# Second attention: scores in two float32r passes over stacked halves, queries made ready once per token tile

## The chip, the cores and the metric

The kernel runs on one core of a Trainium2 chip. Its time is the device time of one execution in microseconds (us). The engines are TensorE (PE, with its weight loads shown apart as PEld), VectorE (DVE), ScalarE (ACT), GpSimd (POOL) and SyncE (SP, which issues most DMAs). PE's granted clock is near its upper level for the whole span (0.996 of 2.4 GHz).

## What is computed

Two transformer blocks follow each other on 512 tokens of 1024 features, all in float32: a first block (convolution, stick-breaking attention, attention over a memory, gates, MLP), then an attention layer, a gated feed-forward layer, a state-space layer, and another feed-forward layer. The change is in the attention layer of the second part, which has two kinds of eight heads of 64 each:

```
    qa = rmsnorm(heads(qa, H_A), q_norm_a)
    ka = rmsnorm(heads(ka, H_A), k_norm_a)
...
    oa = band_attention(qa, ka, heads(va, H_A), A_PREV_CHUNKS, bias_a, None)
    qb = rmsnorm(heads(qb, H_B), q_norm_b)
    kb = rmsnorm(heads(kb, H_B_KV), k_norm_b)
...
    bias_b = (-slopes[:, None, None] * jnp.abs(rel_b).astype(jnp.float32)).reshape(
```

Kind a sees all 512 tokens back, with a bias from a table; kind b sees a window of 128, with a bias of a slope 2^-(h+1) times the distance, a sink in the softmax's denominator, and one key head for four query heads.

## The kernel before

A Python program records every instruction in the order in which its engine will run it. It keeps a clock of its own, with estimated costs, and a heap of generators: each does a few instructions, yields a delay, and is taken up again when that time has come. Weight products are jobs (`jobB`), taken one after the other; between their matmuls `pump` runs what is due in the heap, so the attention's instructions land between the projections' matmuls. Each engine then runs its own queue strictly in order and waits on semaphores where data isn't ready. Weight matmuls (`gb`) take three float32r passes, over weights that ACT (`whi`) and DVE (`wlo`) split into a high and a low part.

The attention layer projects the shared keys and values of kind b, then the queries `qb`, then `ka`, `qa`, `va`, and at last two halves of the output projection for each kind. When a token tile (128 tokens) of a projection is done, `head_norm` (L1338) squares it (`sq`, ACT), sums, takes the root on POOL, scales into `ay` (DVE), has PE transpose it (`at`) and ACT copy it out with the gain (`qb`, `ka`, `qa`, `kbT`). Tiles hold two heads of 64 in 128 partitions.

`units_of` (L1399) makes one unit for each token tile and head, first all of kind b, then all of kind a; `Flow` starts one at least every 1.4 us of the recording's clock (`LA`), up to six at a time. A unit's steps: `sz` masks a pair's query tile into two tiles `qz`, each with the other head's 64 partitions zeroed (`by_head`, L206, on ACT or DVE, whichever the recording believes free); `s0` computes the scores `as` (PE, one float32 matmul) and adds bias and takes the row's minimum in one DVE instruction (`less`, `ae`); `s1` exponentials (ACT); `s2` the reciprocal and the scaling (DVE or ACT); `s3` transposes (`ap`, PE) and copies out (`apT`, ACT); `s4` multiplies with the values (`ao`, PE), whose result is split into `oTh` and `oTl` for the output projection. For kind b the bias table `relB` was multiplied by each head's slope ahead of time, eight ACT instructions into a tile of eight tables.

The first block's stick-breaking attention works otherwise already: `pair_evac` makes tiles `qq` and `kk` in which a head's high part lies in 64 partitions and its low part, or a copy, in the other 64, and its scores `z` are two float32r matmuls. Its rows in the trace are quoted below.

Of the kernel before, what the change touches and what calls it, by code (L numbers as in the profile page):

```python
# [21 lines left out]
KD = 8  # L22
# [21 lines left out]
COLS = {}  # L44
# [27 lines left out]
def kernel(ctx: ExitStack, tc: tile.TileContext, ins: dict, out: bass.AP, parts=(1, 2, 3, 4, 5)):  # L72
# [150 lines left out]
    halves = cp.tile([128, 2], F32, tag="halves", name="halves")  # L223
# [5 lines left out]
    def setup_consts():  # L229
# [3 lines left out]
        for i in range(2):  # L233
            dve.memset(halves[64 * i:64 * i + 64, i:i + 1], 1.0)
            dve.memset(halves[64 - 64 * i:128 - 64 * i, i:i + 1], 0.0)
# [1076 lines left out]
    def attn(G):  # L1312
# [4 lines left out]
        def less(e, s, bias, first, m):  # L1317

            dve.tensor_tensor_reduce(out=e, in0=s, in1=bias, scale=-1.0, scalar=first, op0=ALU.add, op1=ALU.min,
                                     accum_out=m)  # L1320

        def load_rel():
            relB = t2("relB")[:, 0:256]
# [5 lines left out]
            def heads():  # L1329
                dve.tensor_scalar(out=S["sink"], in0=col("sink", 0, 8), scalar1=-1.0, scalar2=None, op0=ALU.mult)  # L1330
                for h in range(8):
                    act.activation(out=S["relB"][:, h * 256:(h + 1) * 256], in_=relB, func=AF.Copy,
                                   scale=2.0 ** -(h + 1))
                    yield 0.6

            spawn(heads(), 4.0)

        def head_norm(src, nh, dst, tt, gname, dup, key):  # L1338
# [12 lines left out]
            dve.tensor_scalar(out=r, in0=r, scalar1=rs, scalar2=None, op0=ALU.mult)  # L1351
            y = t2("ay")
            rb = r.rearrange("p (h o) -> p h o", o=1).to_broadcast([128, nh, 64])
            if dup:
                for i in range(2):
                    dve.tensor_tensor(out=y[:, 0:2 * n].rearrange("p (h i d) -> p h i d", i=2, d=64)[:, :, i, :],
# [663 lines left out]
```

## Time and profile before

| what | us |
|---|---|
| median of 3 runs (2481.61 to 2482.71) | 2482.68 |
| the profiled execution's own time | 2481.79 |
| its span, first to last instruction | 2480.1 |
| PE busy | 2438.7 |
| DVE busy | 1527.0 |
| ACT busy | 1120.3 |

A busy time is the part of the span in which the engine had at least one instruction under way. Consecutive matmuls overlap in the trace: one starts before the end that is shown for the one before it, so a stretch is read from start to start. An idle time is put down to what released the engine.

### The profile page before, as it was taken

How to read it: one execution, taken by the hardware profiler on the slowest of the kernel's cores; microseconds unless marked ns; L12 is line 12 of the kernel's file. 1: busy time of each engine (PE TensorE's matmuls, PEld its weight loads, DVE VectorE, ACT ScalarE, POOL GpSimd, SP SyncE). 2: the span in 40 equal slices, each digit the busy share in tenths (PEclk: the TensorE clock that was granted, in tenths of full speed). 3: DMA queues.
4: the chain of work that ended last, by engine and by line, in shares of the span. 5: the costliest groups of instructions: out<-in, count | busy, mean ns of one | idle time of the engine just before them, and what ended most of it. 6: DMA issues, size and time to landing. Idle time of an engine off the chain costs nothing.

```text
span 2480.1 us, 30728 instructions
## 1 busy us (share of the span) xinstructions
PE 2438.7 (98%) x11556; PEld 1980.8 (80%) x11556; DVE 1527.0 (62%) x2784; ACT 1120.3 (45%) x2410; POOL 248.2 (10%) x303
## 2 busy tenths in 40 slices
PE   8999999999999999999999999999999999999999
PEld 6877877788888888888776888887788887888887
DVE  6436456653444566646756566776698687667674
ACT  6545444432333444545666343333565545433332
POOL 1102011101110011102100000000011011001010
PEclk9999999999999999999999999999999998999999
DMA  6313332333323565622221354442432431245452
GB/s 206 104 57 96 112 100 79 91 106 111 102 89 116 156 166 138 130 89 76 78 72 40 112 136 119 133 97 79 117 106 78 124 115 60 91 147 119 136 111 77
DMA packets 218533, 264.78 MB, mean 107 GB/s; under 512 B 7024, under 2 KB 157936, under 8 KB 218384
## 3 DMA queue, kind: packets, MB, share of 16 engines
q1 hardware_dynamic: 198848, 222.83, 27.9%
q0 software_dynamic: 15232, 29.36, 7.4%
q10 hardware_dynamic: 4304, 10.62, 1.5%
q8 instruction: 91, 1.49, 0.3%
q14 instruction: 58, 0.48, 0.1%
HBM read 254.33 MB, written 4.26 MB: 104 GB/s over the span
## 4 chain that ended last, share of the span: by engine, by line
PE 87%; DVE 5%; issue 4%; ACT 2%; DMA 1%; POOL 0%; ACTq 0%; SPq 0%; POOLq 0%; DVEq 0%
PE ga L87 47%; PE gb L87 21%; PE gw L87 11%; PE y L87 2%; PE as L87 1%; DVE wlo L120 1%; PE o L87 1%; PE tr L92 1%; PE aT L92 1%; PE z L87 1%; PE ao L87 1%; DVE fy L120 1%; PE ap L92 0%; DVE ae L120 0%; PE st L87 0%
## 5 line engine op out<-in xcount | busy, mean ns | idle before, releaser
L87 PE MATMUL ga<-hh,whi 128*128 128x512 f32 x1672 | 661.1, 395 | 0.0
L87 PE MATMUL ga<-hh,wlo 128*128 128x512 f32 x1672 | 652.2, 390 | 0.3 <-DVE wlo L120 0.2
L87 PE MATMUL ga<-hl,whi 128*128 128x512 f32 x1672 | 652.0, 390 | 0.0
L120 DVE TENSOR_TENSOR wlo<-raw,whi 128x512 fp32r<-128x512 f32 x701 | 479.3, 705 | 228.0 <-ACT whi L120 226.1
L120 ACT CAST whi<-raw 128x512 fp32r<-128x512 f32 x701 | 413.2, 617 | 157.2 <-PE ga L87 63.5
L87 PEld LDWEIGHTS ga<-hh,wlo 128*128 128x128 f32 x1672 | 313.6, 188 | 68.0 <-DVE wlo L120 1.2
L87 PEld LDWEIGHTS ga<-hh,whi 128*128 128x128 f32 x1672 | 313.9, 188 | 66.2 <-issue 2.6
L87 PEld LDWEIGHTS ga<-hl,whi 128*128 128x128 f32 x1672 | 314.0, 188 | 64.6 <-issue 1.2
L87 PE MATMUL gb<-whi,hh 128*128 128x512 f32 (+1 forms) x416 | 170.8, 411 | 0.0
L87 PE MATMUL gb<-wlo,hh 128*128 128x512 f32 (+1 forms) x416 | 159.0, 382 | 1.1 <-DVE wlo L120 1.1
L87 PE MATMUL gb<-whi,hl 128*128 128x512 f32 (+1 forms) x416 | 159.7, 384 | 0.0
L120 DVE TENSOR_TENSOR wlo<-b,whi 128x512 fp32r<-128x512 f32 x196 | 131.2, 686 | 36.8 <-ACT whi L120 36.8
L120 ACT ACTIVATE fy<-fy,cols 128x512 f32<-128x512 f32 x60 | 43.5, 725 | 206.5 <-DVE fy L120 206.4
L120 ACT CAST whi<-b 128x512 fp32r<-128x512 f32 x196 | 114.1, 615 | 15.6 <-PE gw L87 11.2
L120 DVE SCALAR_TENSOR_TENSOR x<-gw,rsp,x 128x512 f32<-128x512 f32 x98 | 70.0, 750 | 69.4 <-PE gw L87 69.2
L120 DVE SCALAR_TENSOR_TENSOR fy<-fg,cols,fy 128x510 f32<-128x510 f32 (+1 forms) x136 | 103.4, 760 | 4.8
L120 DVE TENSOR_TENSOR fg<-ga,R 128x512 f32<-128x512 f32 x68 | 46.8, 689 | 80.7 <-PE ga L87 69.8
L87 PEld LDWEIGHTS gb<-whi,hl 128*128 128x128 f32 x416 | 78.2, 188 | 16.0
L87 PEld LDWEIGHTS gb<-wlo,hh 128*128 128x128 f32 x416 | 78.5, 189 | 15.2 <-DVE wlo L120 1.7
L87 PEld LDWEIGHTS gb<-whi,hh 128*128 128x128 f32 x416 | 78.4, 188 | 14.2 <-issue 1.2
L655 POOL DMA_DIRECT2D b<-in_ffn_w_out_dram x32 | 38.5, 1203 | 507.6 <-DVE wlo L120 503.7
L87 PE MATMUL gw<-whi,fss 128*128 128x512 f32 x256 | 81.4, 389 | 0.0
(316 smaller groups left out, 4002.4 us busy)
## 6 DMA issues: line engine op xcount, KB each, us to landing
raw<-in_ffn_w_in_dram SPq DMA_DIRECT2D x44, 1024.0 KB, 5.1
raw<-in_w_in_dram SPq DMA_DIRECT2D x32, 1024.0 KB, 5.1
raw<-in_w_up_dram SPq DMA_DIRECT2D x16, 1024.0 KB, 5.5
b<-in_ffn_w_out_dram POOLq DMA_DIRECT2D x32, 512.0 KB, 5.6
raw<-in_ssm_w_in_dram SPq DMA_DIRECT2D x16, 1024.0 KB, 5.2
b<-in_w_down_dram POOLq DMA_DIRECT2D x24, 512.0 KB, 6.1
b<-in_ffn_w_out_dram SPq DMA_DIRECT2D x12, 1024.0 KB, 8.0
b<-in_w_down_dram SPq DMA_DIRECT2D x9, 1024.0 KB, 7.9
```

The source lines that it names most:

```text
L87: nc.tensor.matmul(o, lhsT=lhsT, rhs=rhs, **kw)
L92: nc.tensor.transpose(o, i, idn)
L120: return fn(*args, **kw)
L655: nc.gpsimd.dma_start(out=r3(R[nm][:, a * 512:(c + 1) * 512], c + 1 - a), in_=dram(i, j, a, c + 1), accum_op=ALU.add)
```

## The change

Scores of the second attention are computed in two float32r passes instead of one float32 matmul. The key tiles (`put_k`) hold, for each of the two heads, the high part in that head's 64 partitions (ACT) and the low part in the other 64 (DVE). The queries keep their transposed float32 tile (`put_q`), and a new generator `queries` makes, once for each token tile and kind, a tile `qq`: for each of the two heads ACT casts the high part, DVE subtracts to get the low part, and a DMA issued from ACT copies both into the other 64 partitions. It is spawned at the first unit of a kind for tile 0, and in the third head pair of a tile for the next; `s0` waits for it in the recording's clock. `by_head` and its masks go. The slopes of kind b move: `relB` is one table, the queries are multiplied by 2^(h+1) in the scaling that was there (by a tile `slope` set once by eight GpSimd memsets), and `less` multiplies the sum by -2^-(h+1) instead of -1. The key tile of kind b is no longer doubled ahead of its transposes (one transpose in place of two).

```diff
-    def by_head(q):
-
-        z = t2("qz")[:, 0:256]
-        for g in range(2):
-            o, h = z[:, g * 128:(g + 1) * 128], halves[:, g:g + 1]
-            if lighter(dve, act, 0.0) is act:
-                act.activation(out=o, in_=q, func=AF.Copy, scale=h)
-            else:
-                dve.tensor_scalar(out=o, in0=q, scalar1=h, scalar2=None, op0=ALU.mult)
-        return z
...
-            S["relB"] = u8("relB8")
...
+            S["slope"] = cp.tile([128, 8], F32, tag="slope", name="slope")
+            for h in range(8):
+                pool.memset(S["slope"][:, h:h + 1], 2.0 ** (h + 1))
...
+        def put_k(key):
+
+            def put(ps, tt):
+                for g in range(2):
+                    hi, lo = slice(64 * g, 64 * g + 64), slice(64 - 64 * g, 128 - 64 * g)
+                    t = r3(S[key][g], ps.shape[1])
+                    gain = cols[hi, COLS[key + "g"]:COLS[key + "g"] + 1]
+                    c = slice(tt * 128, tt * 128 + 128)
+                    act.activation(out=t[hi, :, c], in_=ps[hi], func=AF.Copy, scale=gain)
+                    dve.scalar_tensor_tensor(out=t[lo, :, c], in0=ps[hi], scalar=gain, in1=f(t[hi, :, c]),
+                                             op0=ALU.mult, op1=ALU.subtract)
+            return put
+
+        def queries(kind, tt):
+
+            while ("q" + kind, tt) not in S:
+                yield 0.3
+            t = u8("qq", F32R)
+            q = r3(S["q" + kind], 4)[:, :, tt * 128:tt * 128 + 128]
+            for g in range(2):
+                hi, lo = slice(64 * g, 64 * g + 64), slice(64 - 64 * g, 128 - 64 * g)
+                a = g * 1024
+                act.copy(r3(t[:, a:a + 512], 4)[hi], q[hi])
+                dve.tensor_sub(r3(t[:, a + 512:a + 1024], 4)[hi], q[hi], f(r3(t[:, a:a + 512], 4)[hi]))
+                act.dma_start(out=f(t[lo, a:a + 1024]), in_=f(t[hi, a:a + 1024]))
+            yield 3.0
+            S["qq" + kind, tt] = t
...
+        def score(ps, q, k, pr, g):
+            for i in range(2):
+                o = g * 1024 + i * 512 + pr * 128
+                pe.matmul(ps, lhsT=q[:, o:o + 128], rhs=k, start=i == 0, stop=i == 1)
...
-                        def sz(pr=pr, tt=tt, c=c, g=g):
-                            if g == 0:
-                                c["q"] = by_head(S["q" + kind][:, pr * 512 + tt * 128:pr * 512 + tt * 128 + 128])
+                        def sz(pr=pr, tt=tt, g=g):
+                            if g == 0 and pr == 0 and tt == 0:
+                                spawn(queries(kind, 0))
+                            if g == 0 and pr == 2 and tt < 3:
+                                spawn(queries(kind, tt + 1))
...
-                                pe.matmul(S_, lhsT=q, rhs=S["kb"][:, o:o + n], start=True, stop=True)
-                                less(e, S_, S["relB"][:, h * 256 + 256 - n:h * 256 + 256], S["sink"][:, h:h + 1], m)
+                                score(S_, q, S["kb"][pr // 2][:, t0 * 128:t0 * 128 + n], pr, g)
+                                less(e, S_, S["relB"][:, 256 - n:256], S["sink"][:, h:h + 1], m, 2.0 ** -(h + 1))
...
-            a = small("acol", 32)
+            a = t2("acol")[:, 0:32]
```

What moves is shown at three places. On PE at the start of kind b: `at` are the transposes of a query tile, `gb` the weight matmuls (here of the projection of `ka`), `as` the scores. Before, from the first tile's transposes on:

```order
L92 MATMUL at<-ident,ay 128x128 x4
L87 MATMUL gb<-whi_0_9857,hh_9322 128x512
L87 MATMUL gb<-wlo_0_9858,hh_9322 128x512
L87 MATMUL gb<-whi_0_9857,hl_9323 128x512
L87 MATMUL gb<-whi_1_9880,hh_9322 128x512
L87 MATMUL gb<-wlo_1_9881,hh_9322 128x512
L87 MATMUL gb<-whi_1_9880,hl_9323 128x512
L87 MATMUL as<-kbT,qz 128x128
```

Now twelve weight matmuls follow the first tile's transposes, and then, from the second tile's transposes on:

```order
L92 MATMUL at<-ident,ay 128x128 x4
L87 MATMUL gb<-whi_0_9857,hh_9317 128x512
L87 MATMUL gb<-wlo_0_9858,hh_9317 128x512
L87 MATMUL gb<-whi_0_9857,hl_9318 128x512
L87 MATMUL gb<-whi_1_9880,hh_9317 128x512
L87 MATMUL gb<-wlo_1_9881,hh_9317 128x512
L87 MATMUL gb<-whi_1_9880,hl_9318 128x512
L87 MATMUL as<-kb,qq 128x128 x6
```

The first score moved from behind 6 weight matmuls to behind 18 and another tile's transposes, and three heads' scores (two passes each) stand together there.

On ACT at the same place (`sq` are squares of later tiles, `whi` weight casts, `ae` exponentials; in brackets whom an instruction waits for). Before:

```order
L120 ACTIVATE qb<-at,cols 128x4x128 [waits PE_49]
L120 ACTIVATE sq<-gb,asc 128x512 [waits DVE_49]
L120 CAST whi_1_9994<-raw_9855 128x512 [waits Activation_49]
L120 ACTIVATE qb<-at,cols 128x4x128 [waits PE_49]
L120 ACT_TABLE_LOAD [waits DVE_49]
L120 ACTIVATE ae,sd<-ae,sm 128x128 [waits Activation_49]
```

Now:

```order
L120 ACTIVATE qb<-at,cols 128x4x128 [waits PE_49]
L120 ACTIVATE sq<-gb,asc 128x512 [waits DVE_49]
L120 CAST qq<-qb 64x512 [waits Activation_49]
L1377 DMA qq<-qq 64x1024 [waits DVE_49]
L120 CAST qq<-qb 64x512
L1377 DMA qq<-qq 64x1024 [waits DVE_49]
L120 CAST whi_1_9998<-raw_9855 128x512
L120 ACTIVATE qb<-at,cols 128x4x128 [waits PE_49]
```

Two casts and two DMAs stand ahead of the weight cast, and each DMA waits in ACT's queue for DVE.

On ACT at the start of kind a, around the first eviction of a value tile (`va`). Before:

```order
L120 ACTIVATE va<-gb,rs 128x512 [waits PE_49]
L120 ACTIVATE ae,sd<-ae,sm 128x128 [waits DVE_49]
L120 COPY apT<-ap 128x128 [waits PE_49]
L120 CAST oTh_10194<-ao 128x128 [waits PE_49]
L120 CAST whi_2_11274<-raw_10873 128x512
```

Now:

```order
L120 ACTIVATE va<-gb,rs 128x512 [waits DMAHW1_49,DMAHW0_49,PE_49]
L120 ACTIVATE ae<-ae,sd 128x256 [waits DVE_49,Activation_49]
L120 CAST qq<-qa 64x512
L1377 DMA qq<-qq 64x1024 [waits DVE_49]
L120 CAST qq<-qa 64x512
L1377 DMA qq<-qq 64x1024 [waits DVE_49]
L120 CAST whi_2_11225<-raw_10815 128x512
L120 COPY apT<-ap 128x256 [waits PE_49]
```

Kind a's first query tile is made behind the first value tile's eviction; before, kind a's first exponentials stood there already. On PE, 18 weight matmuls and eight small ones (four `ao`, four `ap`) stand between the end of that value tile and kind a's first scores.

## Rows read from the trace of the kernel before

**Rows 1.** The page's busy times, share of the span, and instructions.

```profile
PE 2438.7 (98%) x11556; PEld 1980.8 (80%) x11556; DVE 1527.0 (62%) x2784; ACT 1120.3 (45%) x2410; POOL 248.2 (10%) x303
```

**Rows 2.** Stretches: us, then busy PE, PEld, DVE, ACT, POOL; clock, DMA share, GB/s.

```profile
1164.00:1259.00 95.00, 93.82 (x533) 73.31 (x531) 68.29 (x274) 67.70 (x216) 16.96 (x10) 1.00 0.22 74
1259.00:1349.00 90.00, 83.43 (x490) 59.39 (x489) 51.58 (x192) 57.02 (x162) 0.00 (x0) 1.00 0.18 59
```

**Rows 3.** Groups by form, 1160 to 1350 us, score records: count, busy us, mean ns.

```profile
L87 PE MATMUL as<-kbT,qz 128*128 128x256 f32 x48 | 14.0, 386 | 1.2 <-DVE sd L120 1.1
L87 PE MATMUL as<-ka,qz 128*128 128x512 f32 x16 | 8.5, 612 | 0.6 <-ACT qz L120 0.6
...
L87 PE MATMUL as<-ka,qz 128*128 128x384 f32 x16 | 6.8, 505 | 1.3 <-ACT qz L120 1.3
L87 PE MATMUL as<-ka,qz 128*128 128x256 f32 x16 | 4.8, 384 | 0.0
```

**Rows 4.** Groups by form, 190 to 540 us: the first block's scores.

```profile
L87 PE MATMUL z<-kk,qq 128*128 128x512 f32 x32 | 11.0, 424 | 0.0
L87 PE MATMUL z<-kk,qq 128*128 128x384 f32 x32 | 9.0, 362 | 0.0
L87 PE MATMUL z<-kk,qq 128*128 128x256 f32 x32 | 6.5, 286 | 0.0
```

**Rows 5.** Timeline of PE, 1163 to 1167 us: start, us, instruction.

```profile
1163.41 0.60 PE L92 MATMUL at<-ident,ay 128*128 128x128 f32 x4
1163.76 0.48 PE L87 MATMUL gb<-whi,hh 128*128 128x512 f32 x1
```

**Rows 6.** Waits of PE, 1150 to 1350 us: total, times, longest.

```profile
PE gb L87 <- DVE oTl L120: 2.5, 3, 1.7
PE gb L87 <- ACT oTh L120: 2.2, 3, 1.0
PE as L87 <- ACT qz L120: 2.0, 3, 1.1
```

**Rows 7.** Timeline of ACT, 196 to 204 us: start, us, instruction, idle before.

```profile
196.33 0.59 ACT L120 ACTIVATE qq<-ga 64x512 fp32r<-64x512 f32 x1 [2.99 <-PE ga L87]
197.67 0.52 ACTq L1079 DMA_DIRECT2D qq<-qq  x1
198.24 0.59 ACT L120 ACTIVATE qq<-ga 64x512 fp32r<-64x512 f32 x1 [1.31 <-DVE qq L120]
199.59 0.47 ACTq L1079 DMA_DIRECT2D qq<-qq  x1
200.10 1.14 ACT L120 CAST whi<-raw 128x512 fp32r<-128x512 f32 x2 [1.27 <-DVE qq L120]
201.77 0.58 ACT L120 CAST kk<-ga 64x512 fp32r<-64x512 f32 x1 [0.53 <-PE ga L87]
203.11 0.58 ACT L120 CAST kk<-ga 64x512 fp32r<-64x512 f32 x1 [0.75 <-DVE kk L120]
203.71 0.62 ACT L120 CAST whi<-raw 128x512 fp32r<-128x512 f32 x1
```

**Rows 8.** Groups by form of ACT, 1130 to 1350 us: the masks.

```profile
L120 ACT ACTIVATE qz<-qa,halves 128x128 f32<-128x128 f32 x16 | 5.7, 395 | 0.0
L120 ACT ACTIVATE qz<-qb,halves 128x128 f32<-128x128 f32 x11 | 4.1, 400 | 0.0
```

**Rows 9.** The chain that ended last, 1160 to 1180 us: start, us, what.

```profile
1167.70 1.39 PE gb L87 x6
```

**Rows 10.** Timeline of ACT, 1163 to 1166 us.

```profile
1164.04 0.69 ACT L120 ACTIVATE qb<-at,cols 128x512 f32<-128x512 f32 x1 [1.96 <-PE at L92]
1164.63 0.68 ACT L120 ACTIVATE sq<-gb,asc 128x512 f32<-128x512 f32 x1
1165.20 0.62 ACT L120 CAST whi<-raw 128x512 fp32r<-128x512 f32 x1
```

**Rows 11.** DMA issues: count, KB each, us from issue to landing.

```profile
qq<-qq ACTq DMA_DIRECT2D x16, 256.0 KB, 2.9
```

**Rows 12.** Waits of ACT, 1164 to 1259 us: total, times, longest.

```profile
ACT apT L120 <- PE ap L92: 8.9, 9, 2.5
```

More of the change, by code (lines that the diff above doesn't have):

```diff
@@ L1315, in attn, with less @@
         oT = {}
-        def less(e, s, bias, first, m):
-            dve.tensor_tensor_reduce(out=e, in0=s, in1=bias, scale=-1.0, scalar=first, op0=ALU.add, op1=ALU.min,
+        def less(e, s, bias, first, m, scale=1.0):
+            dve.tensor_tensor_reduce(out=e, in0=s, in1=bias, scale=-scale, scalar=first, op0=ALU.add, op1=ALU.min,
                                      accum_out=m)
         def load_rel():
-            relB = t2("relB")[:, 0:256]
+            relB = S["relB"] = cp.tile([128, 256], F32, tag="relB", name="relB")
             act.dma_start(out=relB, in_=ins["relB"])
@@ L1326, in load_rel, with head_norm @@
             S["sink"] = cp.tile([128, 8], F32, tag="nsink", name="nsink")
-            S["relB"] = u8("relB8")
[L1329 to L1338, printed above, removed]
+            dve.tensor_scalar(out=S["sink"], in0=col("sink", 0, 8), scalar1=-1.0, scalar2=None, op0=ALU.mult)
+            S["slope"] = cp.tile([128, 8], F32, tag="slope", name="slope")
+            for h in range(8):
+                pool.memset(S["slope"][:, h:h + 1], 2.0 ** (h + 1))
+        def head_norm(src, nh, put, tt, key):
             n = nh * 64
@@ L1365, in head_norm, with put_q @@
             ps = bank("t", "at")
-            for q in range(np_):
+            for q in range(nh // 2):
                 pe.transpose(ps[:, q * 128:(q + 1) * 128], y[:, q * 128:(q + 1) * 128], ident)
-            act.activation(out=r3(dst[:, 0:np_ * 512], np_)[:, :, tt * 128:tt * 128 + 128],
-                           in_=r3(ps[:, 0:np_ * 128], np_), func=AF.Copy, scale=col(gname))
+            put(r3(ps[:, 0:nh * 64], nh // 2), tt)
             rel("t")
             S[key, tt] = True
-        def ev_norm(key, gname):
+        def put_q(key):
+            def put(ps, tt):
+                act.activation(out=r3(S[key], 4)[:, :, tt * 128:tt * 128 + 128], in_=ps, func=AF.Copy,
+                               scale=col(key + "g"))
+            return put
@@ L1421, in s0 @@
                                     load_bias(0)
-                                k = S["ka"][:, pr * 512:pr * 512 + n]
-                                pe.matmul(S_, lhsT=q, rhs=k, start=True, stop=True)
+                                k = S["ka"][g][:, pr * 512:pr * 512 + n]
+                                score(S_, q, k, pr, g)
                                 far = max(0, n - 256)
@@ L1485, in units_of @@
                         s0.need, s3.need, s4.need = ("t", 1), ("t", 1), ("t", g)
+                        s0.when = lambda tt=tt: ("qq" + kind, tt) in S
                         sz.when = lambda tt=tt: ("q" + kind, tt) in S and ("k" + kind, tt) in S
```

38 lines of the change are left out of this document (16 added, 22 removed).

## The prediction

> **What bounds the kernel now.** I read the page first: TensorE (PE) is busy for 98% of the span [rows 1], so at most places only less PE work, or less PE waiting, shows in the time. Then I cut out the stretch that the change can touch, from the first use of the transposed queries (1164 us) to the last product with the values (1349 us). Until 1259 us the attention runs between the projections' matmuls: PE idles 1.2 of 95 us, while ScalarE (ACT) works 67.7 us, 71%. In the other 90 us PE idles 6.6 us and ACT works 57.0 [rows 2]. So the first part is PE's, and the second is PE's with waits; ACT is second in both. PE's order is fixed by the recording, so whatever stands next in its queue and isn't ready stops everything behind it.
>
> **PE work removed.** A float32 score leaves two records in the trace, a float32r pair leaves two as well, and the first block's scores already have exactly the form that the change brings (tiles `kk`, `qq`). So the saving per record is the difference of two means [rows 3, 4]: 256 columns 386 - 286 = 100 ns for 48 records of kind b (4.8 us) and 98 ns for 16 of kind a (1.6), 384 columns 143 ns x 16 = 2.3, 512 columns 188 ns x 16 = 3.0. At 128 columns I take nothing. Further, four transposes go, since a key tile of two heads is no longer doubled: four of them hold PE for 1163.76 - 1163.41 = 0.35 us [rows 5]. Sum: **-12.0 us**. The waits for the masked queries `qz` go too, 2.0 us [rows 6]: **-2.0**.
>
> **What the queries now cost ACT.** The first block shows the new chain on ACT in order of time [rows 7]: cast at 196.33, VectorE (DVE) subtracts, the DMA that copies the half tile to the other 64 partitions is issued at 197.67, second cast at 198.24, second DMA at 199.59, next work at 200.10. The DMA stands in ACT's own queue and waits there for DVE, so one token tile holds ACT for 200.10 - 196.33 = 3.77 us, of which only two casts of 0.59 are work. Behind it stand the exponentials, the copies out of PSUM and the casts of the weights. Eight such tiles: 30.2 us. The keys' two half casts take turns with DVE as well: 203.11 - 201.77 = 1.34, twice 0.6 and 0.75 between, about 1.94 us for the 0.59 pitch of one cast now; 1.35 more for each of four `ka` tiles, 5.4 us. Gone are 11 + 16 masks `qz` on ACT, 11 x 0.400 = 4.4 and 16 x 0.395 = 6.3 us [rows 8]. The eight `relB` products that go lie earlier, under projections in which PE doesn't wait, so they count for nothing; if that cover failed they would be a small gain. DVE gains and loses alike (21 + 16 masks away, 16 + 8 half-tile subtractions in) and I book nothing for it; were it late, it would lengthen the holds just named. The slopes cost nothing in the bias instruction: it already multiplies by -1, and the eight memsets on GpSimd come once, ahead of the first scores. `acol` in another pool moves no work.
>
> Before 1259 us ACT's load becomes 67.7 + 4 x 3.77 + 5.4 - 4.4 = 83.8 us beside 93.8 - 5.2 = 88.6 us of PE work, 95% instead of 71%; after it 57.0 + 15.1 - 6.3 = 65.8 beside 83.4 - 6.9 = 76.5, 86%.
>
> **Where PE will wait.** At the start of kind b: in the new order PE has, between the first tile's transposes (1163.41) and the first scores, 12 weight matmuls, four transposes, 6 weight matmuls: 0.35 + 2 x 1.39 + 0.35 + 1.39 [rows 5, 9] puts it there at 1168.3. ACT is at the transposed tile at 1164.04, at the squares at 1164.63, at the first cast at 1165.20 [rows 10]; by the pitches of [rows 7] the second half's DMA is issued at 1165.20 + 1.91 + 1.35 = 1168.5, and lands 2.9 us later [rows 11], at 1171.4. The second score needs it: **+3.1 us**. The bounds are 0 (were ACT that much earlier) and 5 (were DVE behind by two instructions of 0.7).
>
> The Trainium skill's page "DMA: Bandwidth & Descriptors" (section "Anatomy of one DMA") gives a copy about 2.0 us fixed plus its bytes at 436 GB/s, fitted for the GpSimd path: for 256 KB an estimate of 2.6. The row says 2.9 on ACT's path, and the row is used; by the page this wait and the next would each be 0.3 us shorter.
>
> At the start of kind a the tile's cast stands behind the first value eviction and one scaling. With V the end of the first value tile on PE, ACT reaches the first cast at V + 0.59 + 0.41, and the second half lands at V + 1.0 + 1.91 + 1.35 + 2.9 = V + 7.2. PE has 18 weight matmuls (3 x 1.39) and eight small ones (about 0.09 each) until the scores, V + 4.9: **+2.3 us**, bounds 0 and 5 as before.
>
> The other six tiles are asked for two head pairs ahead, and their landing is covered. But each still holds ACT for 3.8 us, and the scalings and copies behind it come later by that much less the slack they had. The trace shows that slack only on one side: in this stretch ACT was nine times ahead of PE's transposes, by about 1 us each [rows 12]. I take 4 us in all for these six and for the keys: 0 if the slack covers it, 16 if all of ACT's idle time of the first part (95 - 67.7 = 27.3) is forced and is added to 83.8, which makes 111 of 95. The low end is nearer, as PE idles only 1.2 us there now: **+4.0**.
>
> Sum: -12.0 - 2.0 + 3.1 + 2.3 + 4.0 = -4.6 us, from the profiled execution's own 2481.79 to 2477.2; the median of before lies 0.9 above that execution, so **2478.1**.
>
> **Rivals.** (1) Everything is hidden: the queries are ready when PE comes, and the 14.0 us stay: 2468.7. For it speaks that the first block's tiles of this kind, with the same holds, sit under PE without a wait for `qq`; against it that there the scores come several microseconds after the copies, here 4.9 after the transposes. The page named above (section "Rules for kernel authors") says to issue a DMA early and wait late, so that its fixed cost overlaps; by that rule this is what should come, if the issue were early.
>
> (2) No net gain: the 6.9 us saved after 1259 us fall where PE waits for others anyway, 6.6 us of idle [rows 2], for results of ACT and DVE [rows 6]. Then -12.0 - 2.0 + 6.9 + 3.1 + 2.3 + 4.0 = +2.3, 2485.0.
>
> (3) Slower: ACT becomes the bound until 1259 us. The place is the query and key tiles between 1164 and 1220 us; the part then lasts 83.8 us plus what idle time of ACT is forced. The second part gains 6.9 + 2.0 - 2.3 = 6.6, so the kernel is slower once the forced idle passes 95 + 6.6 - 83.8 = 17.8 of the 27.3 us. With 25: +7.2, 2489.9. Against it: part of that idle is ACT waiting for PE, which shrinks when PE is the one that waits.
>
> That the two passes are no cheaper than the four is ruled out by [rows 4].
>
> **How the numbers follow.** Forecast 45% (its own range 2474 to 2481.5), all hidden 17%, no net gain 23%, slower 15%. A measurement of this kernel tells about 0.2%, 5 us, from no change. Faster by more than that: rival 1 and a little under half of the forecast, 38%; slower: rival 3 and a sliver of rival 2, 16%; same 46%. The range 2468.5 to 2487 takes in the forecast, rival 2 and most of rival 1, and the near edge of rival 3.
>
> **What would show it.** Records `as<-kb,qq` and `as<-ka,qq` with means like those of `z`; 2 to 4 us of PE idle before the first of each, released by the DMA on `qq`; ACT idle for about 1.3 us before the second cast and before what follows, released by DVE `qq`, 16 times; PE idle for `ae`, `apT` or `oTh` between 1170 and 1220 us. Wrong would be: PE idle at both starts under 1 us, or PE's waits in the first part above 15 us.

## The result, and the profile after

The changed kernel takes **2499.96 us** (median of 4 runs, 2493.92 to 2500.66); before takes 2482.69 in the same comparison (4 runs, 2481.61 to 2483.91). The ratio is **1.0061**, interval 1.0047 to 1.0075: slower by 17 us, where 4.6 us faster was forecast, and outside the range. The profiled execution is one of 2500.66 us, span 2499.0.

First I asked where the 19 us between the two profiled executions lie. I took two points that both programs have: the first transposes of kind b's queries (`at`, at 1163.41 before and 1164.37 after) and the first `ga` matmul of what follows the attention (1363.00 and 1382.77). The stretch between them grew from 199.6 to 218.4 us; the rest of the span differs by 0.1. Two windows of after cover this stretch, cut at the first scores of kind a (columns as in [rows 2]); the page's line of busy times stands ahead of them:

```profile
PE 2438.9 (98%) x11552; PEld 1983.8 (79%) x11552; DVE 1536.1 (61%) x2764; ACT 1125.8 (45%) x2406; POOL 247.3 (10%) x311
```

```profile
1164.37:1278.90 114.53, 100.47 (x544) 78.86 (x542) 72.28 (x246) 74.57 (x217) 16.73 (x10) 0.93 0.29 85
1278.90:1382.77 103.87, 92.44 (x551) 70.38 (x551) 64.89 (x218) 63.68 (x177) 1.11 (x2) 0.97 0.24 70
```

The page shows nothing: PE 98% as in [rows 1]. The windows show two things. PE is idle for 14.1 and 11.4 us, 25.5 in all; over the same stretch of before it was 8.1. And the granted clock, 1.00 in both windows of [rows 2], is 0.93 and 0.97. ACT, which I feared as the bound, is busy 65% and 61%. So ACT isn't short of time, it is late. The waits of PE say for what (1150 to 1390 us; total, times, longest):

```profile
PE ap L92 <- ACT apT L120: 4.9, 1, 4.9
PE gb L87 <- ACT oTh L120: 4.5, 5, 1.8
PE ap L92 <- ACT ae L120: 3.6, 4, 1.4
PE gb L87 <- DVE oTl L120: 3.2, 3, 1.4
PE as L87 <- DMA qq<-qq: 2.5, 2, 1.5
```

Beside [rows 6], `qz` is gone and `qq`'s landing has come, as forecast. New are the waits for ACT's copies and exponentials, 4.9 us of it in one piece. Its history on ACT (start, us, instruction, idle before it):

```profile
1207.68 0.61 ACT L120 CAST qq<-qb 64x512 fp32r<-64x512 f32 x1
1209.04 0.47 ACTq L1377 DMA_DIRECT2D qq<-qq  x1
1209.55 0.61 ACT L120 CAST qq<-qb 64x512 fp32r<-64x512 f32 x1 [1.26 <-DVE qq L120]
1210.92 0.47 ACTq L1377 DMA_DIRECT2D qq<-qq  x1
1211.43 0.62 ACT L120 CAST whi<-raw 128x512 fp32r<-128x512 f32 x1 [1.26 <-DVE qq L120]
1211.95 0.68 ACT L120 ACTIVATE ka<-at,cols 64x512 fp32r<-64x512 f32 x1
1213.44 0.68 ACT L120 ACTIVATE ka<-at,cols 64x512 fp32r<-64x512 f32 x1 [0.81 <-DVE ka L120]
1214.15 0.37 ACT L120 COPY apT<-ap 128x256 f32<-128x256 f32 x1
```

One query tile holds ACT from 1207.68 to 1211.43, 3.75 us, of which the two casts are 1.22. That is the hold of [rows 7] to 0.02 us. The two half casts of a key tile follow with DVE between them, and only then comes the copy that PE waits for. On PE:

```profile
1214.57 0.69 PE L92 MATMUL ap<-ident,ae 128*128 128x128 f32 x2 [4.87 <-ACT apT L120]
1214.91 0.77 PE L87 MATMUL gb<-whi,hh 128*128 128x512 f32 x1
1215.48 0.63 PE L87 MATMUL gb<-wlo,hh 128*128 128x512 f32 x1
1215.91 0.63 PE L87 MATMUL gb<-whi,hl 128*128 128x512 f32 x1
```

The weight matmuls behind the wait start 0.43 us apart, where six of them took 1.39, 0.23 each, before [rows 9]. Windows of 4 us, around the first wait for `qq` and around this one, show the granted clock (the third column from the right):

```profile
1168.00:1172.00 4.00, 1.96 (x10) 1.23 (x8) 2.95 (x6) 2.44 (x4) 1.62 (x1) 1.00 0.61 131
1172.00:1176.00 4.00, 3.59 (x11) 3.04 (x12) 2.75 (x11) 1.23 (x2) 0.01 (x1) 0.52 0.38 83
1176.00:1180.00 4.00, 4.00 (x19) 3.59 (x18) 1.89 (x8) 2.15 (x3) 0.00 (x0) 0.63 0.23 48
...
1208.00:1212.00 4.00, 1.70 (x10) 1.20 (x8) 1.40 (x3) 1.48 (x4) 0.63 (x1) 1.00 0.31 66
1212.00:1216.00 4.00, 1.43 (x5) 1.24 (x6) 2.52 (x6) 2.35 (x6) 0.00 (x0) 0.64 0.31 66
1216.00:1220.00 4.00, 2.96 (x10) 2.27 (x9) 2.17 (x4) 2.83 (x8) 0.00 (x0) 0.50 0.00 0
1220.00:1224.00 4.00, 4.00 (x15) 3.24 (x16) 2.69 (x10) 1.50 (x3) 0.00 (x0) 0.58 0.33 73
```

PE idles in both places, and the clock then stands at the lower of its levels (0.5, 1.2 GHz) for some microseconds, in which the weight matmuls take nearly twice as long. In before, with no wait over 1.7 us [rows 6], this doesn't occur in the stretch. But the length of a wait alone doesn't decide it: after's wait of 2.19 us until `apT`, which ends at 1245.06, has the full clock behind it, and so has the longest wait of b_only (a run described below), here with two windows in columns as above:

```profile
1234.29 0.50 PE L87 MATMUL gb<-whi,hh 128*128 128x512 f32 x1 [2.77 <-DVE ay L120]
```

```profile
1232.00:1236.00 4.00, 1.71 (x9) 1.40 (x9) 3.79 (x17) 0.80 (x2) 1.64 (x1) 1.00 0.36 141
1236.00:1240.00 4.00, 4.00 (x25) 3.38 (x24) 3.38 (x12) 3.71 (x13) 1.64 (x1) 1.00 0.01 4
```

Behind which waits the clock falls, no run here settles.

### The profile page after: what moved, and what is told of

The parts are those of the page before. It is cut to its first block, busy times and chain, and to the rows that moved or that the text cites. A ratio compares the mean times of both kernels' runs of the same rounds, so it can differ in the third digit from the quotient of the medians.

```text
span 2499.0 us, 30718 instructions
## 1 busy us (share of the span) xinstructions
PE 2438.9 (98%) x11552; PEld 1983.8 (79%) x11552; DVE 1536.1 (61%) x2764; ACT 1125.8 (45%) x2406; POOL 247.3 (10%) x311
## 4 chain that ended last, share of the span: by engine, by line
PE 86%; DVE 5%; issue 4%; ACT 2%; DMA 1%; POOL 0%; ACTq 0%; SPq 0%; POOLq 0%; DVEq 0%
PE ga L87 47%; PE gb L87 20%; PE gw L87 11%; PE y L87 2%; DVE wlo L120 1%; PE o L87 1%; PE tr L92 1%; PE aT L92 1%; PE z L87 1%; PE ao L87 1%; DVE fy L120 1%; PE as L87 1%; PE ap L92 0%; ACT ae L120 0%; DVE ae L120 0%
## 5 line engine op out<-in xcount | busy, mean ns | idle before, releaser
L120 ACT CAST whi<-b 128x512 fp32r<-128x512 f32 x196 | 114.1, 616 | 15.6 <-PE gw L87 11.2
L87 PEld LDWEIGHTS gb<-whi,hl 128*128 128x128 f32 x416 | 79.5, 191 | 16.4
```

The lines of the kernel that those rows point to most:

```text
L87: nc.tensor.matmul(o, lhsT=lhsT, rhs=rhs, **kw)
L120: return fn(*args, **kw)
```

## A ledger of the stretch

Each row of this table is one profiled execution, cut at the same two points into 100 windows; it lay up to 3 us under the median of its runs (pool_issue, key_order), in b_whole2 2 us above. Idle is the length less PE's busy time; lost to the clock is the sum of busy time x (1 - granted clock); work is busy time less that, PE's work at full clock. The last columns are the median of all runs and the ratio to before in the same comparison.

| kernel | length | idle | lost to clock | work | time, us | ratio, interval |
|---|---|---|---|---|---|---|
| before | 199.6 | 8.1 | 0.0 | 191.5 | 2482.69 | |
| after | 218.4 | 25.5 | 10.1 | 182.8 | 2499.96 | 1.0061 [1.0047, 1.0075] |
| before_unused | 217.9 | 21.2 | 2.9 | 193.8 | 2500.80 | 1.0070 [1.0055, 1.0085] |
| unused_pool | 205.1 | 11.2 | 1.7 | 192.2 | 2487.42 | 1.0017 [1.0008, 1.0026] |
| pool_issue | 210.1 | 20.5 | 7.3 | 182.2 | 2491.95 | 1.0035 [1.0023, 1.0046] |
| late_issue | 205.5 | 19.2 | 2.9 | 183.4 | 2486.89 | 1.0017 [1.0008, 1.0027] |
| key_order | 214.2 | 24.8 | 6.4 | 183.0 | 2496.19 | 1.0058 [1.0041, 1.0075] |
| late_key | 203.4 | 18.3 | 1.7 | 183.4 | 2485.83 | 1.0010 [1.0001, 1.0019] |
| late_key_long | 211.3 | 21.7 | 5.7 | 183.9 | 2494.42 | 1.0050 [1.0033, 1.0067] |
| one_query | 203.3 | 18.6 | 3.3 | 181.4 | 2486.03 | 1.0013 [1.0003, 1.0022] |
| no_low_keys | 201.8 | 16.4 | 4.5 | 180.8 | 2484.51 | 1.0008 [0.9999, 1.0017] |
| a_only | 207.8 | 15.6 | 6.5 | 185.6 | 2488.66 | 1.0027 [1.0017, 1.0037] |
| b_only | 199.7 | 11.7 | 0.0 | 188.0 | 2483.20 | 1.0007 [0.9998, 1.0016] |
| before_slopes | 199.5 | 8.1 | 0.0 | 191.4 | 2482.82 | 1.0004 [0.9995, 1.0013] |
| filled | 215.2 | 23.8 | 6.6 | 184.7 | 2497.98 | 1.0059 [1.0045, 1.0073] |
| whole2_act | 215.2 | 22.0 | 11.3 | 181.8 | 2494.39 | 1.0040 [1.0026, 1.0053] |
| whole2_pool | 203.6 | 19.0 | 4.2 | 180.3 | 2487.32 | 1.0018 [1.0009, 1.0027] |
| b_whole2 | 222.3 | 23.5 | 11.3 | 187.5 | 2503.18 | 1.0083 [1.0069, 1.0097] |
| wpool_4 | 220.8 | 28.5 | 10.3 | 181.9 | 2500.92 | 1.0076 [1.0064, 1.0089] |
| wpool_6 | 215.9 | 24.0 | 8.8 | 183.1 | 2497.10 | 1.0066 [1.0052, 1.0079] |

From before to after: work -8.7, idle +17.4, clock +10.1, together the 18.8 us. The theories put to the test: **1**, ACT's queue is held by copies that wait in it for DVE, and the clock makes PE's waits dearer; **2**, the query tiles land late; **3**, PE's new order of instructions costs the time, whoever issues the copies.

## Experiments: the holds of ACT's queue

**before_unused** puts the new query tiles into the kernel before, at the same places, and nothing reads them. **unused_pool** is the same with one word changed. Apart from the copies, PE, ACT and DVE run the same instructions in the same order in these two; PE's order differs from before's in the stretch, although the expectation of before_unused takes it to be that of before.

```diff
# before_unused: before, with queries() of the change and the move of acol (not shown), and
+                            if g == 0 and pr == 0 and tt == 0:
+                                spawn(queries(kind, 0))
+                            if g == 0 and pr == 2 and tt < 3:
+                                spawn(queries(kind, tt + 1))
# unused_pool: before_unused, and in queries()
-                act.dma_start(out=f(t[lo, a:a + 1024]), in_=f(t[hi, a:a + 1024]))
+                pool.dma_start(out=f(t[lo, a:a + 1024]), in_=f(t[hi, a:a + 1024]))
```

> The kernel before, its float32 scores with masked queries as they were, plus the new query tiles `qq` (casts, subtractions and copies issued from ACT, at the same places as in the changed kernel), which nothing reads. It measures the holds alone: no PE work is removed and PE waits for no copy. Theory 1: ACT gets 8 holds of 3.8 us more and gives PE its results late; the time rises by 8 to 20 us over before, to 2490 to 2503, with a lower granted clock after the longest waits. Theories 2 and 3: PE's order and its operands are those of before, so within 3 us of before, 2480 to 2486.

> The kernel before with the unused query tiles, with their copies issued from GpSimd's queue instead of ACT's; casts, subtractions and copies stay, and PE's order is the same as in the run with them on ACT's queue, which came 18 us above before. If the hold of ACT's queue is what costs, at least half of the 18 goes: 2484 to 2491. If the added work itself (16 casts of about 0.6 us on ACT, 16 subtractions of about 0.7 us on DVE) is what costs: 2495 to 2502.

Without any saving and without a reader, eight tiles cost 18 us; issued from GpSimd's queue they cost 4.4. Casts, subtractions, copies and the three engines' orders are the same. So 13.4 us come from the copies' place in ACT's queue alone, and the 4.4 from the added work and PE's changed order together, which no run here separates. The waits of PE, 1150 to 1390 us, first with the copies on ACT:

```profile
PE as L87 <- ACT qz L120: 9.0, 8, 3.4
PE as L87 <- DVE sm L120: 2.5, 2, 1.3
PE gb L87 <- DVE oTl L120: 2.1, 3, 0.9
```

and on GpSimd:

```profile
PE as L87 <- ACT qz L120: 5.2, 6, 2.3
PE gb L87 <- DVE oTl L120: 2.1, 3, 0.9
PE gb L87 <- ACT oTh L120: 1.6, 3, 0.8
```

What is late most of all is `qz`, a product that has nothing to do with the query tiles but stands behind them in ACT's queue.

**pool_issue** is the same one word in the changed kernel, again with the same order on PE, ACT and DVE. **late_issue** leaves the copies on ACT and records them after both casts and both subtractions:

```diff
                 act.copy(r3(t[:, a:a + 512], 4)[hi], q[hi])
                 dve.tensor_sub(r3(t[:, a + 512:a + 1024], 4)[hi], q[hi], f(r3(t[:, a:a + 512], 4)[hi]))
+            yield 0.1
+            for g in range(2):
+                hi, lo = slice(64 * g, 64 * g + 64), slice(64 - 64 * g, 128 - 64 * g)
+                a = g * 1024
                 act.dma_start(out=f(t[lo, a:a + 1024]), in_=f(t[hi, a:a + 1024]))
             yield 3.0
```

> The changed kernel, with the two copies of each query half tile issued from GpSimd's queue instead of ACT's; nothing else, and PE's order is the same. Theory 1 (the copies stand in ACT's queue and wait there for DVE's subtraction, some 1.3 us twice per tile and 16 times in all; what ACT owes to PE comes late, PE idles, and after each idle of several us the granted clock falls): ACT's idle time before `whi` and before the second cast, released by DVE `qq`, falls from some 15 us to under 4, PE's wait for `apT` of 4.9 us goes, PE's idle between 1164 and 1383 us falls from 25.5 us to under 14, and the time to 2478 to 2490. Theory 2 (the copies land late and PE waits for them; ACT's holds are harmless): the waits of PE for `qq` stay or grow, since GpSimd's queue issues them no earlier, and the time stays at 2495 to 2505. Theory 3 (the new order of PE's instructions costs the time, whoever issues): 2495 to 2505 as well, with waits of PE in the same places, `apT` among them.

> The changed kernel, with both casts and both subtractions of a query tile recorded first and the two copies after them, still in ACT's queue; so ACT waits for DVE at most once per tile, late, and does the second cast while DVE subtracts. Theory 1 (holds of ACT's queue): about half to two thirds of the gain of the issue from GpSimd, 2482 to 2493, with ACT's waits for DVE `qq` at 2 to 6 us instead of 15. Theory 2 (late landing): the first half's copy is issued later than now, PE's waits for `qq` grow by 0.5 to 2 us, and the time is 2500 or above. Theory 3 (order): 2495 to 2505.

Both move toward theory 1, and pool_issue less than expected: it is 8.0 us faster than after (late_issue 13.1), but its idle time is 20.5 us, where under 14 was expected, and a wait for `apT` stays. In after, ACT idles 10.3 us before `qq` and 3.8 before `whi`, both released by DVE `qq`; in pool_issue and in late_issue no wait of ACT is released by it. The 4.9 us wait is 2.4 in pool_issue; in late_issue PE waits 4.3 at this place, now until DVE's `ka` (below), and not for ACT. A small part of what pool_issue doesn't give back is the landing: GpSimd's copies land in 3.3 us instead of 2.9, and PE waits 4.0 us for `qq` instead of 2.5. Theory 3 falls as the whole cause with pool_issue and unused_pool, where PE's order is the same and the time isn't; in the 9.2 us that pool_issue still lies above before, the order can have a part. late_issue alone would not separate the two, as it moves the first scores of kind b behind twelve more weight matmuls and four transposes.

**one_query** makes one query tile for each kind, which all token tiles use:

```diff
-            S["qq" + kind, tt] = t
+            for j in range(4):
+                S["qq" + kind, j] = t
...
-                            if g == 0 and pr == 2 and tt < 3:
-                                spawn(queries(kind, tt + 1))
```

> The changed kernel, but each kind makes one query tile only and all four token tiles use it (so the scores of the later token tiles are of other queries): all of PE's saving stays, six of the eight holds of ACT go, with their casts and subtractions. Theory 1 (holds): the time falls under that of before, to 2470 to 2480 (the 2468.7 with all hidden, and the waits at the two starts). Theory 3 (the new order, or two-pass scores that save nothing in place): 2490 or above. If the saving of the second part goes into waits for ACT's `oTh` in any case: 2478 to 2484.

A miss for theory 1 as I had it: 2486.03, not 2470 to 2480. Taking six of eight holds away brings about what late copies bring, 13.9 us, and no more. PE's order changes here too. PE's work is 10 us below before, and PE idles 18.6. So something else than the holds keeps PE waiting, and this is the second half of the answer.

## Experiments: what is left without the holds

**key_order** records the keys' two half casts first and DVE's two subtractions after them; **late_key** is that with late_issue; **late_key_long** waits longer in the recording as well:

```diff
# key_order
                     act.activation(out=t[hi, :, c], in_=ps[hi], func=AF.Copy, scale=gain)
+                for g in range(2):
+                    hi, lo = slice(64 * g, 64 * g + 64), slice(64 - 64 * g, 128 - 64 * g)
+                    t = r3(S[key][g], ps.shape[1])
+                    gain = cols[hi, COLS[key + "g"]:COLS[key + "g"] + 1]
                     dve.scalar_tensor_tensor(out=t[lo, :, c], in0=ps[hi], scalar=gain, in1=f(t[hi, :, c]),
# late_key_long
-            yield 3.0
+            yield 7.0
```

> The changed kernel, with the keys' two half casts on ACT one after the other and DVE's two subtractions behind them, instead of in turns. Theory 1: the turns held ACT for 0.75 us at each of four `ka` tiles and each of four `kb` tiles; that is 3.4 us of ACT's waits before `ka`, and the time falls by 2 to 6 us, to 2494 to 2498, mostly by the 4.9 us wait for `apT`, in whose chain one `ka` hold stands. Theories 2 and 3: no change by more than 2 us, 2498 to 2502.

> The changed kernel, with both edits of the runs before in one: the copies of a query tile recorded behind both casts and both subtractions, and the keys' two half casts ahead of their two subtractions. In the run with the late copies alone PE still idled 4.3 and 1.9 us in the stretch where ACT and DVE take turns at the `ka` tiles. If these turns are what is left to gain there, those waits fall under 2 us in sum and the time is 2479 to 2484. If the turns only happened to end last there and DVE is late in any case, the time stays at 2485 to 2489.

> As the run with both edits, and the recording waits 7.0 instead of 3.0 until it takes a query tile for ready, so that the first scores of each kind stand later in PE's order. Theory 2 (PE waits for landings): another 2 to 5 us faster. Theory 1 (holds): no wait for a landing is left to be saved, so within 2 us of the run with both edits, or 1 to 4 us slower, because the last scores and what follows them come later.

key_order is 3.8 us below after, with intervals that overlap; its runs came in two pairs, 2493.0 twice with a mean clock of 0.994 and 2499.4 and 2499.7 with 0.991. In after itself one run of 2493.92 has 0.994 and three of 2499.76 to 2500.66 have 0.991 or 0.992. The program is the same in each; 0.003 of 2490 us is 7.5. So the clock is large enough for the spread between runs of one kernel; that it is the cause is not shown. On top of late copies the keys' order brings 1.1 us, with overlapping intervals and less than expected: the turns ended last, but DVE is late in any case. late_key_long goes against theory 2: with no wait for a landing left, recording the scores later only moves the waits to the end, 8.6 us slower where theory 1 expected at most 4 (waits for `oTh` and `oTl` 13.4 us).

The wait that stayed, in late_key, on PE:

```profile
1208.02 0.41 PE L92 MATMUL ap<-ident,ae 128*128 128x128 f32 x2 [4.25 <-DVE ka L120]
```

and the two rows of DVE's timeline ahead of it:

```profile
1203.80 1.39 DVE L120 TENSOR_TENSOR qq<-qb,qq 64x512 fp32r<-64x512 f32 x2 [1.14 <-ACT qq L120]
1206.36 1.51 DVE L120 SCALAR_TENSOR_TENSOR ka<-at,cols,ka 64x512 fp32r<-64x512 f32 x2 [1.18 <-ACT ka L120]
```

No copy holds ACT here. A query tile and a key tile come together: two casts on ACT from 1203.16, two subtractions on DVE, two casts, two subtractions until 1207.87, 4.7 us in a row, and by the profile it is the last of them that releases PE's next transposes.

**no_low_keys** is late_issue without the keys' low parts. **a_only** and **b_only** are late_issue with one kind changed and the other as before.

```diff
# no_low_keys
-                    dve.scalar_tensor_tensor(out=t[lo, :, c], in0=ps[hi], scalar=gain, in1=f(t[hi, :, c]),
-                                             op0=ALU.mult, op1=ALU.subtract)
...
+                            pool.memset(f(S[key][g][64 - 64 * g:128 - 64 * g]), 0.0)
# b_only (a_only with the kinds exchanged)
-                            q = S["qq" + kind, tt]
+                            q = c["q"][:, g * 128:(g + 1) * 128] if kind == "a" else S["qq" + kind, tt]
...
-                                score(S_, q, k, pr, g)
+                                pe.matmul(S_, lhsT=q, rhs=k, start=True, stop=True)
```

> The changed kernel with late copies, and the low parts of the keys left out: zeros are written there once by GpSimd, DVE does no subtraction for the keys and ACT's two half casts follow each other (so the scores lack the keys' low part). If ACT and DVE in turns at the key tiles, with the transposes' PSUM bank held meanwhile, cause the 4.3 and 1.9 us of PE idle between 1203 and 1220 us: these go and the time is 2476 to 2482. If they only end last there: 2485 to 2489.

> Only kind b is changed (two-pass scores, query tiles with late copies, slopes in the bias instruction); kind a keeps its float32 scores, masked queries and one-piece keys. If the saving of kind a goes into PE's waits for `oTh` and its key turns and query tiles cost PE waits between 1200 and 1225 us (rival 2 of the prediction, and the key term): faster than the late copies alone, 2477 to 2483. If kind a's saving of 6.9 us in the scores is real on the path: slower than the late copies alone, 2488 to 2494.

> Only kind a is changed (keys in two parts, two-pass scores, query tiles with late copies; the slopes are applied in the new way too); kind b keeps its float32 scores with masked queries and doubled keys. If kind a's part is what costs, by key turns between 1200 and 1225 us and waits for `oTh`: 2486 to 2492, no faster than the late copies alone. If kind b's part is what costs: 2477 to 2483.

no_low_keys falls between its two expectations, 2.4 us below late_issue: the two waits of 4.3 and 1.9 us for `ka` go, and new are waits of 1.8 us for `apT`, at 1201 us, and 3.3 for `oTh`, at 1310. b_only is level with before, a_only 6 us slower. (Three of b_only's ten runs took 2487 us, with a mean clock of 0.992 or 0.993; the profiled one took 2482.91.) Their work falls by 3.5 and 5.9 us, their idle time rises by 3.6 and 7.5. In kind b the saving is paid back exactly; in kind a it is paid back and the clock comes on top (6.5). b_only is 3.7 us faster than late_issue with both kinds, 0.2 above the range that was expected. That kind a's part costs is as expected; the place is not the one that rival 2 names. PE idles 7.2 us in a_only ahead of kind a's first scores, 1.2 in before, and 8.5 behind them, 6.9 in before. So 6.0 of the 7.5 us lie in the first part, with waits of 3.9 us for `qz` at 1200 us and 2.0 for `ka` at 1215, while ACT and DVE make the halves of the key tiles (1194 to 1220).

**before_slopes** is the edit of the slopes alone, in the kernel before:

```diff
-                                less(e, S_, S["relB"][:, h * 256 + 256 - n:h * 256 + 256], S["sink"][:, h:h + 1], m)
+                                less(e, S_, S["relB"][:, 256 - n:256], S["sink"][:, h:h + 1], m, 2.0 ** -(h + 1))
```

> The kernel before with the edit of the slopes alone: one bias tile that the bias instruction scales per head, slopes multiplied into the norm factors of the queries of kind b, `acol` in the other pool; scores as before. All theories: within 2 us of before, 2481 to 2485; eight products on ACT go that lay under busy PE.

No change, 0.1 us in the stretch. It costs nothing and brings nothing.

## Experiments: is it ACT's and DVE's work, and is it the clock?

The casts of half tiles take as long as those of whole ones: 64 partitions x 512 take 0.61 us, 128 x 512 (`whi`) 0.62; a half key tile 0.682 us, a whole one in before 0.690. On DVE a half query tile's subtraction takes 0.687 us, that of a whole weight tile (`wlo`) 0.685. So halves double ACT's and DVE's time for these tiles. **whole2_act** casts and subtracts whole tiles into `qh`, `ql`, `kh`, `kl`, and more copies bring the parts to their halves; **whole2_pool** issues the query copies from GpSimd; **b_whole2** does it for kind b alone.

```diff
# whole2_act; whole2_pool has pool for act in the last line
-                act.copy(r3(t[:, a:a + 512], 4)[hi], q[hi])
-                dve.tensor_sub(r3(t[:, a + 512:a + 1024], 4)[hi], q[hi], f(r3(t[:, a:a + 512], 4)[hi]))
...
+            act.copy(r3(h, 4), q)
+            dve.tensor_sub(r3(l, 4), q, f(r3(h, 4)))
+            yield 0.1
+            for g in range(2):
+                own = slice(64 * g, 64 * g + 64)
+                for s, p in ((0, h), (512, l)):
+                    for i in range(2):
+                        act.dma_start(out=f(t[64 * i:64 * i + 64, g * 1024 + s:g * 1024 + s + 512]), in_=f(p[own]))
```

> The changed kernel with one cast on ACT and one subtraction on DVE for a whole query tile or key tile (128 partitions) instead of two each for halves; eight copies of 128 KB per query tile, issued late from ACT, and four per key tile, issued from GpSimd, bring the parts to their halves. ACT's and DVE's work for these tiles is halved: some 8 casts of 0.6 us and 8 subtractions of 0.7 for the queries, and as much for the keys. If PE's remaining idle comes from ACT's and DVE's work: PE's idle in the stretch falls from 18 us to under 13, the clock stays up, and the time is 2476 to 2482, below before. If not (the order of the recording, or PE and its banks): 2484 to 2488.

> As the run with whole-tile casts and subtractions, with the eight copies of a query tile issued from GpSimd's queue, not ACT's. If the issues cost ACT something or wait there: 1 to 4 us faster than that run. If GpSimd's issues are late, PE waits for `qq` at the two starts, and it is 2 to 6 us slower.

> Kind b alone changed, with whole-tile casts and subtractions as in the run beside it; kind a as before. Against the run with kind b alone and half tiles (2483.2): if ACT's and DVE's work is what PE waits for, 2478 to 2481; if not, 2482 to 2485.

whole2_act and b_whole2 miss both their expectations, and test something else than I meant. ACT in whole2_act, at the first tile:

```profile
1165.28 1.13 ACTq L1382 DMA_DIRECT2D qq<-qh  x2
1166.44 1.26 ACTq L1382 DMA_DIRECT2D qq<-ql  x2
1167.74 1.26 ACTq L1382 DMA_DIRECT2D qq<-qh  x2
1169.03 1.27 ACTq L1382 DMA_DIRECT2D qq<-ql  x2
1170.35 0.69 ACT L120 ACTIVATE qb<-at,cols 128x512 f32<-128x512 f32 x1 [4.58 <-DMA qq<-qh]
```

Eight issues stand in ACT's queue for 5.0 us, some 0.63 each, and ACT does nothing for 4.58 of them, more than in the old hold. In whole2_pool ACT is free of them; PE's order is the same, and it is 7.1 us faster. Its waits of PE are:

```profile
PE as L87 <- DMA qq<-ql: 6.5, 4, 3.6
PE as L87 <- DMA qq<-qh: 4.1, 3, 2.3
PE gb L87 <- ACT oTh L120: 3.7, 4, 1.5
```

Of 19.0 us idle 10.6 are for landings, and all the others 8.4, against 8.1 in before. This speaks for ACT's and DVE's work as what was left, and for a price that went to the landing instead, as GpSimd issues the eight copies 0.51 us apart. It doesn't show it: PE's order isn't that of late_issue, and while PE waits for a landing ACT and DVE have time to come up. Two runs tried to have both, with four copies of 256 KB per query tile (`qp` holds both parts) and the first tile taken for ready later:

```diff
-                for s, p in ((0, h), (512, l)):
...
+                    pool.dma_start(out=f(t[64 * i:64 * i + 64, g * 1024:g * 1024 + 1024]), in_=f(p[own, 0:1024]))
-            yield 3.0
+            yield 4.0 if tt == 0 else 3.0
```

> The changed kernel with whole-tile casts and subtractions for queries and keys, the parts brought to their halves by four copies of 256 KB per query tile and four of 128 KB per key tile, all from GpSimd's queue, and the first query tile of each kind taken for ready 4.0 instead of 3.0 after its copies are recorded. If the remaining loss was the landing: PE's waits for `qq` fall from 10.6 us to 3 to 6, the time to 2474 to 2482. If the saved PE work goes into other waits in any case: 2484 to 2489.

> As the run beside it, with 6.0 for the first tile of each kind, so that 12 more weight matmuls stand ahead of the first scores. If the landing is what is left: waits for `qq` under 3 us and 1 to 3 us faster than the run beside it. If the later scores only move the waits to the end of kind a, as in the run with both edits and 7.0: 3 to 8 us slower than the run beside it.

Both miss: wpool_4 is 0.76% above before, and PE waits 14.2 us for `qq` in it. The copies got slower, not faster. The DMA issues of wpool_4 (count, KB each, median us from issue to landing):

```profile
qq<-qp POOLq DMA_DIRECT2D x32, 256.0 KB, 4.6
```

and of pool_issue:

```profile
qq<-qq POOLq DMA_DIRECT2D x16, 256.0 KB, 3.3
```

Twice the bytes move per tile, as in whole2_pool, whose copies of 128 KB landed in 3.1 to 3.4 us. wpool_6 is 3.8 us below wpool_4; its copies landed in 5.3, and it has 5.4 us of these waits left and 13.0 for `oTh` and `oTl`.

**filled** puts ten matmuls that nothing uses where PE waited 0.9 and 1.5 us for the first tile:

```diff
+                            if kind == "b" and tt == 0 and h < 2:
+                                for _ in range(4 + 2 * h):
+                                    pe.matmul(S_, lhsT=S["kb"][0][:, 0:128], rhs=S["kb"][0][:, 0:512], start=True, stop=True)
```

> The changed kernel, with ten matmuls of 512 columns whose results nothing uses put ahead of the first two scores of kind b (four and six), where PE waited 0.9 and 1.5 us for the query tile's landing and the granted clock then fell: `gb` had a pitch of 0.43 us instead of 0.23 from 1173 to 1179 us. If PE's idling there makes the clock fall: the granted clock of 1172 to 1180 us is 0.9 to 1.0 instead of 0.5 to 0.67, the 24 matmuls run at the pitch 0.23, and this stretch ends 2 to 4 us earlier; the kernel 2494 to 2498, as far as later waits don't absorb it. If the clock falls for another reason (the kind of work, the time since the kernel's start): the same low clock in the same place, and 2498 to 2502.

Its windows of 4 us, columns as above:

```profile
1168.00:1172.00 4.00, 3.90 (x21) 2.79 (x20) 3.12 (x7) 1.83 (x3) 1.64 (x1) 1.00 0.46 97
1172.00:1176.00 4.00, 2.46 (x11) 2.03 (x11) 3.25 (x14) 2.43 (x4) 0.00 (x0) 0.76 0.61 131
1176.00:1180.00 4.00, 4.00 (x19) 3.31 (x18) 2.22 (x12) 3.99 (x17) 0.00 (x0) 0.82 0.00 0
```

PE doesn't idle until 1172.28, and then once, 1.54 us, for DVE `sm`. The low clock comes behind that wait and costs half as much: 1172 to 1180 reads 0.76 and 0.82 instead of 0.52 and 0.63. So the fall moves with the idle time, as expected if PE's idling makes it fall; PE's order behind the ten matmuls changed as well. Filling one wait didn't abolish it, since the next was uncovered, and the kernel's 2.0 us are within the spread of the runs. The Trainium skill's page "TensorE: Matmul & The Clock Gate" (section "HAM oscillation — how this bites in real kernels") says that waits for DMA make the clock fall again and again within a kernel, and puts the penalty at half of the time at the low level. The traces agree that the clock falls again within a kernel, here also behind waits for ACT and DVE, and not behind every one (b_only's 2.77 us). Of the penalty they show the weight matmuls, 0.43 us apart instead of 0.23. The ledger doesn't test it, as it counts the loss from the granted clock: after has 23.9 us at that level, and 10.1 are lost in them, a little under half, as PE is idle in a part.

## Why the prediction was wrong

- **PE's work, -12.0 and 0.35 in it:** the sign right, the size short: -8.7 by the ledger, -7.6 to -11.2 in the other kernels with both kinds changed (filled, with its ten matmuls more, aside). The wide records are as forecast (late_key, groups by form as in [rows 3]); those of 256 columns, 318 and 303 ns, save 68 and 81 instead of 100:

```profile
L87 PE MATMUL as<-kb,qq 128*128 128x256 f32 x48 | 11.3, 318 | 0.7 <-ACT apT L120 0.6
L87 PE MATMUL as<-ka,qq 128*128 128x512 f32 x16 | 5.2, 419 | 0.0
L87 PE MATMUL as<-ka,qq 128*128 128x384 f32 x16 | 4.4, 358 | 0.0
L87 PE MATMUL as<-ka,qq 128*128 128x256 f32 x16 | 3.5, 303 | 0.0
```

  By these rows 3.3 + 3.1 + 2.4 + 1.3 = 10.1 us, where the first block's rows had given 11.7. The 0.35 of the four transposes can't show in the stretch: the key tiles of kind b are transposed before it, at 1140 to 1148 us in before. That the ledger has 8.7 and not 10.1 stays open.
- **Waits for `qz`, -2.0:** gone, as said.
- **Start of kind b, +3.1:** 2.45 (0.93 + 1.52), by the steps foreseen. **Start of kind a, +2.3:** 1.4, but released by a weight cast on ACT, not by the tile:

```profile
1170.48 0.41 PE L87 MATMUL as<-kb,qq 128*128 128x128 f32 x2 [0.93 <-DMA qq<-qq]
1172.41 1.09 PE L87 MATMUL as<-kb,qq 128*128 128x128 f32 x4 [1.52 <-DMA qq<-qq]
1280.70 0.92 PE L87 MATMUL as<-ka,qq 128*128 128x128 f32 x6 [1.41 <-ACT whi L120]
```

- **The other six tiles and the keys, +4.0 (0 to 16): the step that failed.** By the ledger it is 25.5 - (8.1 - 2.0) - 2.45 - 1.4 = 15.5, the far end of the bounds. I chose near the low end because PE idled only 1.2 us there before, and took that for ACT's slack. It says nothing of slack; it says that ACT just kept up. Some 10 of the 15.5 lie ahead of kind a's first scores, the part whose idle time had given the bounds, and some 5 behind them. What the copies' place in ACT's queue makes of it pool_issue shows: 8.0 us of the time, waits and clock together. The rest is the added work of ACT and DVE or PE's changed order, and stays unseparated.
- **The clock, not in the sum at all, without a reason given: +10.1.** -8.7 - 2.0 + 3.9 + 15.5 + 10.1 = 18.8.
- **The rivals.** Rival 3 named the place and the mechanism, holds of ACT between 1164 and 1220 us, but priced it as ACT's load reaching the stretch's length. ACT is at 65%. A queue that works in order makes PE wait long before its engine is full. My sign of being wrong, over 15 us of PE's waits in the first part, was narrowly missed with 14.1. Rival 2, the saving of kind a falling into waits behind 1259 us, is not what a_only shows: there most of the new idle time lies ahead of kind a's scores. Rival 1 is far off: even with most holds gone or the copies late (one_query, late_issue, late_key) the time stays above before.

**What stays open:** no kernel here beats before; b_only and before_slopes are level with it. That PE's 8 to 10 us would show in the time with ACT and DVE relieved and the tiles landed in time is what the ledger suggests, and no run showed it. Nor does one separate the added work of ACT and DVE from PE's changed order in what is left without the holds.

## What to carry to other kernels

A transfer issued from a compute engine's queue cost that engine here the wait for what is transferred, 1.26 us each; ask what stands behind it, and issue it after all work that doesn't need it, or from a queue that has little else. A saving on the bounding engine is paid out only as far as its feeders run ahead, and an idle time near zero of the bounding engine doesn't tell how far that is; double the feeders' work only after looking at each result's lateness. Count a new wait of PE with the lower clock that can follow: in after 10.1 us on top of 25.5 us of idle time, though not behind every wait.

## What the runs showed of the hardware

Instructions of ACT and DVE on 64 partitions took the time of 128 (casts 0.61 and 0.62 us, subtractions 0.687 and 0.685). An issue took 0.47 us by itself and some 0.63 in a row of eight on ACT's queue, 0.51 on GpSimd's (whole2_act, whole2_pool). Copies of 256 KB from GpSimd landed in 3.3 us, and in 4.6 and 5.3 with twice as many. After some waits of PE of 1.5 to 4.9 us the granted clock fell to 0.5, after others of 2.2 to 2.8 it stayed at 1.00 (after, b_only), and the same program ran 6 us apart with its mean clock at 0.994 or 0.991.
